# The second FFN with its activations stationary and 512 columns of weights moving

## The chip, the cores and the metric

The kernel runs on one core of one Trainium2 chip. The metric is the device time of one execution in microseconds (us); three runs of the kernel before lie between 2185.66 and 2185.99 us, median 2185.8.

TensorE (PE) multiplies: it loads a stationary block of up to 128x128 and streams the columns of a moving operand past it into PSUM. VectorE (DVE) and ScalarE (ACT) work elementwise on 128 partitions, GpSimd (POOL) hardly computes here, and SyncE (SP) issues transfers.

## The reference

One layer of a decoder for 16 meta tokens and 256 tokens (T = 272, D = 2048) in float32: a half-step FFN, a mixer (sparse attention and a gated convolution), and a second half-step FFN. The output has only the 256 tokens. The change is in the second FFN:

```
def rms_norm(x, g):
    y = x * rsqrt(mean(x * x, axis=-1) + EPS)
    return y * g

def swiglu(x, w_gate, w_up, w_down):           # (2048, 5632), (2048, 5632), (5632, 2048)
    return (silu(x @ w_gate) * (x @ w_up)) @ w_down

u = rms_norm(h, ffn2_norm_g)
h = h + 0.5 * swiglu(u, w_gate, w_up, w_down)
return h[:, N_META:]
```

## The kernel before

All activations lie feature-major: `h` is [128 features, 16 blocks of features, 272 tokens]. Each float32 product is made of three: weights and activations are each split into a rounded high part and the rest (`whi`, `wlo`; hi and lo of `act` or `mid`), and hi x hi, hi x lo and lo x hi are added up in PSUM.

The weights come through one stream (`Stream`, lines 61 to 151). Each transfer on SP's queue brings 128 x 2048 floats (1 MB) into one of three raw buffers. A transfer is split in two *steps* of 1024 columns: ScalarE copies the high part (line 108) and VectorE subtracts (line 109) into one of four buffers. `next()` hands out blocks; when a step's blocks are used up it first runs what is due (`early`), one entry of `steps`, then issues the split three steps ahead, then the work put off with `later(fn, lag)`. So the order on each engine is the order in which this Python code issues it, and the steps are its clock.

In the FFNs (`ffn`, lines 378 to 429) the weights are stationary, 128x128 at a time, and the tokens move. In the second one `paired` (lines 273 to 278) sends `whi` against hi and lo of 256 tokens in one matmul of 512 columns, then `wlo` against hi in one of 256, so the two halves of a PSUM tile have to be added by ScalarE and VectorE (`joined`, `add_to`). The 5632 middle features are done in two halves of 22 blocks: for each block a gate tile `pg` and an up tile `pu` (16 blocks of weights each), then, for each of 16 output blocks, `pd` over 22 blocks. The last `pd` uses three matmuls of 256 columns instead (`fmajor`). The mean of squares is summed by TensorE (`norm`, lines 339 to 366, with lag 2) while the first matmuls run on activations that are not yet normalised; `R` is multiplied in afterwards. Finished blocks of `h` go out on POOL's queue, or on SP's once every load is issued (line 928).

The index projection in the mixer already does it the other way round: `tokens` (lines 483 to 495) holds a tile of 128 tokens stationary and moves 512 columns of weights, so that PSUM gets [tokens, features] (`pi`, `pq`).

Of the kernel before, what the change touches and what calls it, by code (L numbers as in the profile page):

```python
# [9 lines left out]
F32 = mybir.dt.float32  # L10
F32R = mybir.dt.float32r
# [7 lines left out]
FF = 5632  # L19
NF = FF // P  # L20
FHALF = NF // 2
SEQ = 256
META = 16
T = META + SEQ
# [130 lines left out]
def tile_decoder_layer(  # L155
# [36 lines left out]
    def ffn_chunks(wgu, wd, skip=0):  # L192
        for c in range(2):
            chunks(wgu, max(skip, c * 2 * FHALF), (c + 1) * 2 * FHALF)
            chunks(wd, c * FHALF, (c + 1) * FHALF)

    st.add(wgu1[0], RAW // P, P, (4, 8))
    ffn_chunks(wgu1, wd1, 1)
    chunks(wk, 0, G)
    st.add(wkw, KD, NKW)  # L200
    chunks(wv, 0, G)
# [3 lines left out]
    chunks(wgc, 0, KD * 3 // 2)  # L205
    chunks(wga, 0, KD * 3 // 2)
    chunks(wo, 0, KD)
    ffn_chunks(wgu2, wd2)

    const.tile([P, 32], F32, name="lead")  # L210
    h = const.tile([P, KD, T], F32, name="h")
# [38 lines left out]
    def mm_tile(name="mm"):  # L250
        return psum.tile([P, 512], F32, name=name, tag="mm")
# [15 lines left out]
    def fmajor(ps, xhi, xlo, n):  # L267

        for k in range(n):
            whi, wlo = st.next()  # L270
            mac(ps, whi, wlo, xhi(k), xlo(k), k == 0, k == n - 1)

    def paired(ps, x, n):

        for k in range(n):
            whi, wlo = st.next()
            nc.tensor.matmul(ps.rearrange("p (a t) -> p a t", a=2), whi, x(k), start=k == 0, stop=False)  # L277
            nc.tensor.matmul(ps[:, :SEQ], wlo, x(k)[:, 0, :], start=False, stop=k == n - 1)  # L278

    def joined(out, ps):  # L280
# [17 lines left out]
    def parts(at):  # L298

        return (lambda k, c0=0, c1=T: act[:, k, 0, at + c0 : at + c1]), (  # L300
            lambda k, c0=0, c1=T: act[:, k, 1, at + c0 : at + c1]
        )

    def next_act(d, gain, c0, at):

        x = h[:, d, c0:]
        g = gain[:, d : d + 1]
        hi, lo = (f(d, c0) for f in parts(at))
        nc.scalar.activation(hi, x, AF.Copy, scale=g)
        nc.vector.scalar_tensor_tensor(lo, x, g, hi.bitcast(F32), op0=ALU.mult, op1=ALU.subtract)  # L310
# [64 lines left out]
                mac(ps[:, :n], whi, wlo, xhi(k), xlo(k), k == 0, k == KD - 1)  # L375
        return four

    def ffn(c0, at, done, wait, starting):
        n = T - c0
        a_hi, a_lo = parts(at)  # L380
        pitch = PITCH if n > SEQ else SEQ
        with tc.tile_pool(name=f"ffn{c0}", bufs=2, reuse_waits="tile") as fp:
            mid = fp.tile([P, FHALF, 2, pitch], F32R, name="mid", bufs=1)
            i_hi, i_lo = (mid[:, :, i, pitch - n :] for i in range(2))
            xhi, xlo = (lambda k: a_hi(k, c0)), (lambda k: a_lo(k, c0))
            pairs = n == SEQ

            def up(ps):
                if pairs:
                    paired(ps, lambda k: act[:, k, :, at + c0 : at + T], KD)  # L390
                else:
                    fmajor(ps[:, :n], xhi, xlo, KD)

            def down(ps, last):
                if pairs and not last:
                    paired(ps, lambda k: mid[:, k, :, :], FHALF)
                else:
                    fmajor(ps[:, :n], lambda k: i_hi[:, k, :], lambda k: i_lo[:, k, :], FHALF)

            def normed(out, ps):  # L400
                if pairs:
                    joined(out, ps)
                    nc.vector.tensor_mul(out, out, R[:, c0:])
                else:
                    nc.vector.tensor_mul(out, ps[:, :n], R[:, c0:])

            def gate(pg, box):
                box["t"] = fp.tile([P, n], F32, name="t")
                normed(box["t"], pg)

            def silu(box):
                box["s"] = fp.tile([P, n], F32, name="s")
                nc.scalar.activation(box["s"], box["t"], AF.Silu)

            def times(pu, box):
                box["v"] = fp.tile([P, n], F32, name="v")
                normed(box["v"], pu)
                nc.vector.tensor_mul(box["v"], box["v"], box["s"])

            norm(c0, wait, mm_tile("norm"))  # L420
            least = st.at + wait + 1
            for c in range(2):
                for f in range(FHALF):
                    box = {}
                    side = int(starting and c == 0 and f < 2)
                    if side:
                        if f == 0:
                            four = start_tiles(n, xhi, xlo)
                        pg, pu = four[2 * f : 2 * f + 2]
                    else:  # L430
                        pg, pu = mm_tile("pg"), mm_tile("pu")
                        up(pg)
                    st.later(lambda pg=pg, box=box: gate(pg, box), 1, least)
                    st.later(lambda box=box: silu(box), 2, least + 1)
                    if not side:
                        up(pu)
                    st.later(lambda pu=pu, box=box: times(pu, box), 1 + side, least + 1)
                    st.later(lambda f=f, box=box: split_into(i_hi[:, f, :], i_lo[:, f, :], box["v"]), 2 + side, least + 2)
                for d in range(KD):
                    pd = mm_tile("pd")  # L440
                    last = d == KD - 1 and c == 1
                    down(pd, last)
                    st.later(lambda d=d, pd=pd, last=last: add_to(h[:, d, c0:], pd, 0.5, pairs and not last))
                    if c == 1:
                        done(d)
            if not starting:
                st.flush()

# [9 lines left out]
    for d in range(KD):  # L458
        st.later(lambda d=d: square(d, 0), 4 + d * 7 // KD)

    def done1(d):
        st.later(lambda: (next_act(d, gains[1], 0, LATER), square(d, 0)), 2)

    ffn(0, LATER, done1, 10, True)


    with ExitStack() as mix:
# [15 lines left out]
        def tokens(ps_of, tts):  # L483

            k = 0
            while k < KD:
                blocks = [st.next()] + st.rest()
                for j in tts:
                    t0, n = TT[j]
                    for i, (whi, wlo) in enumerate(blocks):  # L490
                        xhi, xlo = a_hi(k + i, t0, t0 + n), a_lo(k + i, t0, t0 + n)
                        nc.tensor.matmul(ps_of[j], xhi, whi, start=k + i == 0, stop=False)
                        nc.tensor.matmul(ps_of[j], xhi, wlo, start=False, stop=False)
                        nc.tensor.matmul(ps_of[j], xlo, whi, start=False, stop=k + i == KD - 1)
                k += len(blocks)

        steps = st.steps

# [113 lines left out]

        for i in range(2):
            pi = {j: mm_tile(f"pi{j}") for j in (1, 2)}
            tokens(pi, (1, 2))
# [198 lines left out]

        for i in range(2):
            pq = {j: mm_tile(f"pq{j}") for j in (1, 2)}
            tokens(pq, (1, 2))
# [106 lines left out]
            st.later(lambda d=d: (next_act(d, gains[2], META, LATER), square(d, META)), 2)  # L924


    def done2(d):
        st.later(lambda: (nc.sync if st.n_loaded == len(st.loads) else nc.gpsimd).dma_start(out[d], h[:, d, META:]))

    ffn(META, LATER, done2, 2, False)  # L930


_INS = [
# [26 lines left out]

def _down(w):
    return _chunks(np.concatenate([_tiles(w[: FF // 2], P), _tiles(w[FF // 2 :], P)]))


def _branch(gate, w):
# [26 lines left out]
def _layout(x, meta_tokens, ffn1_norm_g, ffn1_w_gate, ffn1_w_up, ffn1_w_down, mix_norm_g, w_in, q_norm_g,  # L992
# [31 lines left out]
    a["wgu2"] = _pairs(ffn2_w_gate[0], ffn2_w_up[0])  # L1024
    a["wd2"] = _down(ffn2_w_down[0])
    return a


# [17 lines left out]
```

## Time and profile before

| | us |
|---|---|
| three runs, median | 2185.8 |
| the profiled execution | 2185.66 |
| its span, from the first to the last instruction | 2183.9 |
| second FFN, first to last matmul | 1446.4 to 2180.7 |
| TensorE busy | 2175.9 |
| VectorE busy | 1317.1 |
| ScalarE busy | 1015.4 |

In the profile PE is the matmuls and PEld the loads of stationary blocks, which overlap. A row of a timeline gives the start, the length and the engine, then line, operation, output <- inputs and shape, and in brackets the idle time before it and what ended that. Matmuls are pipelined: each lasts longer than the distance to the next, so distances are read from starts. Rows of groups give count, busy time, mean duration in ns and the idle time before.

### The profile page before, as it was taken

The page shows a single profiled execution, that of the slowest core. Times are in us where ns is not written, and L with a number is a line of the kernel's source. Part 1 is how long each engine was busy: PE and PEld are TensorE (multiplying, and loading weights), DVE is VectorE, ACT ScalarE, POOL GpSimd, SP SyncE. Part 2 cuts the span into 40 slices and gives each one's busy share as a digit, 9 for nine tenths or more (in the row PEclk, how much of TensorE's full clock was granted, in tenths as well). Part 3 has the DMA queues.
Part 4 walks back from the last instruction along what each step waited for, and adds up shares of the span by engine and source line. Part 5 has one row for each costly group of instructions (what it writes and reads, how often), then busy time and mean ns, then how long its engine had stood idle before and what let it go on. Part 6 is the DMA issues. An engine that isn't in the chain of part 4 may idle for free.

```text
span 2183.9 us, 34927 instructions
## 1 busy us (share of the span) xinstructions
PE 2175.9 (100%) x14554; PEld 2002.7 (92%) x14554; DVE 1317.1 (60%) x1848; ACT 1015.4 (46%) x1460; POOL 15.4 (1%) x26
## 2 busy tenths in 40 slices
PE   9999999999999999999999999999999999999999
PEld 9999999999999998898988888888888888888888
DVE  7555544455555555686566677676666556666654
ACT  6444433344444445564444555554444444444443
POOL 0000000000000000000000000000000000000000
PEclk9999999999999999999999999999999999999999
DMA  6555455545555445443455555555555555555553
GB/s 248 195 185 176 174 177 183 181 174 175 179 185 176 174 167 182 163 157 135 174 184 184 189 186 184 193 175 192 193 193 188 183 192 190 193 193 190 187 205 132
DMA packets 56894, 397.89 MB, mean 182 GB/s; under 512 B 6560, under 2 KB 7712, under 8 KB 9248
## 3 DMA queue, kind: packets, MB, share of 16 engines
q1 hardware_dynamic: 55872, 393.95, 51.2%
q8 instruction: 114, 1.87, 0.3%
q0 software_dynamic: 576, 1.57, 0.2%
q14 instruction: 44, 0.36, 0.0%
q10 hardware_dynamic: 288, 0.15, 0.0%
HBM read 393.54 MB, written 2.10 MB: 181 GB/s over the span
## 4 chain that ended last, share of the span: by engine, by line
PE 96%; DVE 2%; ACT 1%; DMA 1%; issue 0%; ACTq 0%; DVEq 0%
PE pu L277 7%; PE pg L277 7%; PE pd L277 7%; PE pgt L277 6%; PE pd L264 4%; PE pd L263 4%; PE pd L265 4%; PE pu L263 4%; PE pu L265 4%; PE pu L264 4%; PE pg L263 4%; PE pg L265 4%; PE pg L264 4%; PE pu L278 4%; PE pg L278 4%; PE pd L278 4%
## 5 line engine op out<-in xcount | busy, mean ns | idle before, releaser
L109 DVE TENSOR_TENSOR wlo<-raw,whi 128x1024 fp32r<-128x1024 f32 (+1 forms) x747 | 912.9, 1222 | 794.2 <-ACT whi L108 793.4
L108 ACT ACTIVATE whi<-raw 128x1024 fp32r<-128x1024 f32 (+1 forms) x747 | 788.5, 1056 | 985.8 <-issue 159.9
L277 PE MATMUL pg<-act,whi 128*128 128x512 f32 x704 | 246.3, 394 | 0.4 <-DVE act L310 0.4
L277 PE MATMUL pu<-act,whi 128*128 128x512 f32 x704 | 246.2, 394 | 0.0
L277 PE MATMUL pd<-mid,whi 128*128 128x512 f32 x682 | 236.5, 394 | 0.0
L263 PE MATMUL pd<-mid,whi 128*128 128x272 f32 (+1 forms) x726 | 207.9, 286 | 0.0
L265 PE MATMUL pd<-mid,wlo 128*128 128x272 f32 (+1 forms) x726 | 207.9, 286 | 0.0
L264 PE MATMUL pd<-mid,whi 128*128 128x272 f32 (+1 forms) x726 | 207.9, 286 | 0.0
L278 PE MATMUL pg<-act,wlo 128*128 128x256 f32 x704 | 195.1, 277 | 0.0
L278 PE MATMUL pu<-act,wlo 128*128 128x256 f32 x704 | 195.0, 277 | 0.0
L263 PE MATMUL pg<-act,whi 128*128 128x272 f32 x672 | 192.7, 287 | 0.0
L264 PE MATMUL pg<-act,whi 128*128 128x272 f32 x672 | 192.5, 287 | 0.0
L265 PE MATMUL pu<-act,wlo 128*128 128x272 f32 x672 | 192.5, 287 | 0.0
L264 PE MATMUL pu<-act,whi 128*128 128x272 f32 x672 | 192.5, 287 | 0.0
L265 PE MATMUL pg<-act,wlo 128*128 128x272 f32 x672 | 192.5, 287 | 0.0
L263 PE MATMUL pu<-act,whi 128*128 128x272 f32 x672 | 192.5, 287 | 0.0
L278 PE MATMUL pd<-mid,wlo 128*128 128x256 f32 x682 | 188.9, 277 | 0.0
L277 PE MATMUL pgt<-act,whi 128*128 128x512 f32 x512 | 182.2, 398 | 0.0
L277 PEld LDWEIGHTS pg<-act,whi 128*128 128x128 f32 x704 | 132.0, 188 | 31.4 <-DVE act L310 0.7
L277 PEld LDWEIGHTS pu<-act,whi 128*128 128x128 f32 x704 | 132.0, 188 | 30.6
L277 PEld LDWEIGHTS pd<-mid,whi 128*128 128x128 f32 x682 | 127.9, 188 | 29.7
L278 PE MATMUL pgt<-act,wlo 128*128 128x256 f32 x512 | 143.8, 281 | 0.0
(214 smaller groups left out, 4040.2 us busy)
## 6 DMA issues: line engine op xcount, KB each, us to landing
raw<-in_wgu_dram SPq DMA_DIRECT2D x175, 1024.0 KB, 4.8
raw<-in_wd_dram SPq DMA_DIRECT2D x88, 1024.0 KB, 4.9
raw<-in_wcv_dram SPq DMA_DIRECT2D x24, 1024.0 KB, 4.8
raw<-in_wgc_dram SPq DMA_DIRECT2D x24, 1024.0 KB, 4.7
raw<-in_wga_dram SPq DMA_DIRECT2D x24, 1024.0 KB, 4.7
raw<-in_wo_dram SPq DMA_DIRECT2D x16, 1024.0 KB, 4.8
raw<-in_wqi_dram SPq DMA_DIRECT2D x8, 1024.0 KB, 4.8
raw<-in_wq_dram SPq DMA_DIRECT2D x8, 1024.0 KB, 4.7
```

What stands on the lines that cost most here:

```text
L108: nc.scalar.activation(hi[:, :n], raw, AF.Copy)
L109: nc.vector.tensor_sub(lo[:, :n], raw, hi[:, :n].bitcast(F32))
L263: nc.tensor.matmul(ps, whi, xhi, start=first, stop=False)
L264: nc.tensor.matmul(ps, whi, xlo, start=False, stop=False)
L265: nc.tensor.matmul(ps, wlo, xhi, start=False, stop=last)
L277: nc.tensor.matmul(ps.rearrange("p (a t) -> p a t", a=2), whi, x(k), start=k == 0, stop=False)
L278: nc.tensor.matmul(ps[:, :SEQ], wlo, x(k)[:, 0, :], start=False, stop=k == n - 1)
```

## The change

In the second FFN the activations become stationary and the weights move. `tokens` is lifted out of the mixer and takes any operand: for each step of two 128x512 weight blocks and each of two tiles of 128 tokens, three matmuls of 512 columns per block. Gate, up and down results are now [tokens, features]. So:

- the weights are laid out on the host in tiles of 512 columns; the middle features are done in groups of 6 and then 5 times 512, each group with its own down projection;
- the norm's factor belongs to a partition (`rcol`): ScalarE applies it with Silu straight from PSUM, VectorE in one product with the gate;
- the product `s` [tokens, 512 features] must become [features, tokens] to be stationary for the down projection: VectorE turns squares of 32x32 (`STREAM_TRANSPOSE`), 16 instructions of 32 partitions x 256 for each 512 features, over four steps; then `mid` is split as before;
- the residual `h` is turned the same way into `ht` [tokens, 2048] by 32 instructions of 32 partitions x 512, one at each of 32 steps from the fifth on;
- the output leaves as [tokens, features] in eight transfers of 256 KB, the last ones on SP's and ScalarE's queues.

```diff
+GROUPS = 6, 5
...
+    def tokens(ps_of, x, n):
+        k = 0
+        while k < n:
+            blocks = [st.next()] + st.rest()
+            for j, ps in ps_of.items():
+                for i, (whi, wlo) in enumerate(blocks):
+                    xhi, xlo = x(k + i, j, 0), x(k + i, j, 1)
+                    nc.tensor.matmul(ps, xhi, whi, start=k + i == 0, stop=False)
+                    nc.tensor.matmul(ps, xhi, wlo, start=False, stop=False)
+                    nc.tensor.matmul(ps, xlo, whi, start=False, stop=k + i == n - 1)
+            k += len(blocks)
...
+    def turned(dst, src, rows, cols):
+        nc.vector.transpose(dst[rows * 32 : rows * 32 + 32], src[cols * 32 : cols * 32 + 32])
+
+    def ffn_tokens():
...
+            st.steps.extend([lambda: None] * 4)
+            st.steps.extend(lambda j=j, q=q, r=r: turn_h(j, q, r) for j in range(2) for q in range(4) for r in range(4))
...
+            st.later(lambda: nc.vector.tensor_add(ssq[0][:, META:], ssq[0][:, META:], ssq[1][:, META:]), 2)
+            st.early(across, 3)
+            st.later(root, 3)
+            st.later(inverse, 4)
...
+            def gate(pg, s):
+                for j in (1, 2):
+                    nc.scalar.activation(s[:, j - 1], pg[j], AF.Silu, scale=rcol[:, 2 * j : 2 * j + 1])
+
+            def times(pu, s):
+                for j in (1, 2):
+                    nc.vector.scalar_tensor_tensor(
+                        s[:, j - 1], pu[j], rcol[:, 2 * j : 2 * j + 1], s[:, j - 1], op0=ALU.mult, op1=ALU.mult
+                    )
+
+            def turn_s(mt, s, r):
+                for q in range(4):
+                    turned(
+                        mt.rearrange("p f (j r b) -> p r j f b", j=2, r=4)[:, r],
+                        s.rearrange("p j (f q b) -> p q j f b", f=4, q=4)[:, q],
+                        q, r,
+                    )
+
+            def add(d, j, pd, last):
+                to = ht[:, j - 1, d * 512 : (d + 1) * 512]
+                nc.vector.scalar_tensor_tensor(to, pd, 0.5, to, op0=ALU.mult, op1=ALU.add)
+                if last:
+                    queue = nc.gpsimd if st.n_loaded < len(st.loads) else (nc.sync, nc.scalar)[j - 1]
+                    queue.dma_start(out[j - 1, :, d * 512 : (d + 1) * 512], to)
+
+            for c, n in enumerate(GROUPS):
+                for f in range(n):
...
+                    tokens(pg, act_tokens, KD)
+                    st.later(lambda pg=pg, s=s: gate(pg, s))
+                    pu = {j: mm_tile(f"pu{j}") for j in (1, 2)}
+                    tokens(pu, act_tokens, KD)
+                    st.later(lambda pu=pu, s=s: times(pu, s))
+                    for r in range(4):
+                        st.later(lambda mt=mt, s=s, r=r: turn_s(mt, s, r), 2 + r)
+                    to = mid[:, 4 * f : 4 * f + 4]
+                    st.later(lambda to=to, mt=mt: split_into(to[:, :, 0], to[:, :, 1], mt), 6)
+                for d in range(D // 512):
+                    pd = {j: mm_tile(f"pd{j}") for j in (1, 2)}
+                    tokens(pd, lambda k, j, part: mid[:, k, part, (j - 1) * P : j * P], 4 * n)
+                    for j in (1, 2):
+                        st.later(lambda d=d, j=j, ps=pd[j], c=c: add(d, j, ps, c == 1))
```

On TensorE, at the start of the second FFN, the order before (`po` is the end of the output projection):

```order
L277 MATMUL po<-ms_13662,whi 128x512
L278 MATMUL po<-ms_13662,wlo 128x256
L277 MATMUL pg<-act,whi 128x512
L278 MATMUL pg<-act,wlo 128x256
L277 MATMUL pg<-act,whi 128x512
L278 MATMUL pg<-act,wlo 128x256
```

And now, at the same place (two `pg` tiles, one for each 128 tokens):

```order
L290 MATMUL pg_14727<-whi,act 128x512
L291 MATMUL pg_14727<-wlo,act 128x512
L292 MATMUL pg_14727<-whi,act 128x512
L290 MATMUL pg_14727<-whi,act 128x512
L291 MATMUL pg_14727<-wlo,act 128x512
L292 MATMUL pg_14727<-whi,act 128x512
L290 MATMUL pg_14728<-whi,act 128x512
L291 MATMUL pg_14728<-wlo,act 128x512
L292 MATMUL pg_14728<-whi,act 128x512
```

Pairs of 512 and 256 columns give way to matmuls of 512 columns alone, six in a row for each token tile. On VectorE, the order before for one block of 128 middle features:

```order
L283 TENSOR_TENSOR t<-pg,u 128x256
L403 TENSOR_TENSOR t<-t,R 128x256
L109 TENSOR_TENSOR wlo<-raw,whi 128x1024 x2
L283 TENSOR_TENSOR v<-pu,u 128x256
L403 TENSOR_TENSOR v<-v,R 128x256
L418 TENSOR_TENSOR v<-v,s 128x256
L109 TENSOR_TENSOR wlo<-raw,whi 128x1024
L296 TENSOR_TENSOR mid<-v,mid 128x256
```

And now, after the second 512 middle features, where the last turns of the residual (`ht`) still lie between:

```order
L483 SCALAR_TENSOR_TENSOR s<-pu_15204,rcol,s 128x512
L483 SCALAR_TENSOR_TENSOR s<-pu_15205,rcol,s 128x512
L446 STREAM_TRANSPOSE ht<-h 32x16x32
L110 TENSOR_TENSOR wlo<-raw,whi 128x1024
L446 STREAM_TRANSPOSE mt<-s 32x2x4x32 x4
L446 STREAM_TRANSPOSE ht<-h 32x16x32
L110 TENSOR_TENSOR wlo<-raw,whi 128x1024
L446 STREAM_TRANSPOSE mt<-s 32x2x4x32 x4
L446 STREAM_TRANSPOSE ht<-h 32x16x32
L110 TENSOR_TENSOR wlo<-raw,whi 128x1024
L446 STREAM_TRANSPOSE mt<-s 32x2x4x32 x4
```

The work on the middle features has moved from every block of 128 to a burst after each 512, and between two weight splits stand five turns now.

## Rows read from the trace of the kernel before

**Rows 1.** The page: TensorE's busy time, and the clock row of 40 slices.
```profile
PE 2175.9 (100%) x14554; PEld 2002.7 (92%) x14554; DVE 1317.1 (60%) x1848; ACT 1015.4 (46%) x1460; POOL 15.4 (1%) x26
...
PEclk9999999999999999999999999999999999999999
```

**Rows 2.** Second FFN: length, busy us (count) of PE, PEld, DVE, ACT, POOL; clock, DMA.
```profile
1446.39:2180.71 734.32, 733.64 (x4250) 641.91 (x4248) 449.43 (x600) 340.03 (x474) 6.65 (x12) 1.00 0.53 187
```

**Rows 3.** Timeline, TensorE (start us, us): end of output projection, second FFN.
```profile
1440.03 0.40 PE L277 MATMUL po<-ms,whi 128*128 128x512 f32 x1
...
1446.39 0.40 PE L277 MATMUL pg<-act,whi 128*128 128x512 f32 x1
...
1599.95 0.39 PE L277 MATMUL pu<-act,whi 128*128 128x512 f32 x1
...
1603.42 0.39 PE L277 MATMUL pg<-act,whi 128*128 128x512 f32 x1
...
2180.07 0.28 PE L265 MATMUL pd<-mid,wlo 128*128 128x256 f32 x1
```

**Rows 4.** Timeline, TensorE, index projection: two starts 75 matmuls apart.
```profile
833.10 0.39 PE L492 MATMUL pi<-whi,act 128*128 128x512 f32 x1
...
850.10 0.39 PE L492 MATMUL pi<-whi,act 128*128 128x512 f32 x1
```

**Rows 5.** Groups by shape, TensorE (count, busy us, mean ns, idle before).
```profile
L277 PE MATMUL pg<-act,whi 128*128 128x512 f32 x704 | 246.3, 394 | 0.4 <-DVE act L310 0.4
...
L277 PE MATMUL pu<-act,whi 128*128 128x512 f32 x704 | 246.2, 394 | 0.0
...
L277 PE MATMUL pd<-mid,whi 128*128 128x512 f32 x682 | 236.5, 394 | 0.0
...
L263 PE MATMUL pd<-mid,whi 128*128 128x256 f32 x22 | 6.2, 283 | 0.0
```

**Rows 6.** Groups by shape, VectorE.
```profile
L109 DVE TENSOR_TENSOR wlo<-raw,whi 128x1024 fp32r<-128x1024 f32 x743 | 909.8, 1225 | 792.2 <-ACT whi L108 791.5
...
L292 DVE TENSOR_TENSOR h<-h,u 128x256 f32<-128x256 f32 x47 | 20.0, 425 | 22.4 <-ACT u L291 22.4
...
L770 DVE COPY pTm<-ppt 16x256 f32<-16x256 f32 x8 | 3.3, 410 | 1.2 <-ACT pTx L769 0.9
...
L296 DVE TENSOR_TENSOR ys<-ppv,ys 128x512 fp32r<-128x512 f32 x4 | 2.8, 691 | 2.9 <-ACT ys L295 2.9
...
L331 DVE RECIPROCAL rs_y<-rs_z 128x256 f32<-128x256 f32 x1 | 1.7, 1744 | 0.0
```

**Rows 7.** Groups by shape, ScalarE.
```profile
L108 ACT ACTIVATE whi<-raw 128x1024 fp32r<-128x1024 f32 x743 | 785.8, 1059 | 982.4 <-issue 159.9 <-PE pd L264 144.4 <-PE pg L264 141.9
...
L413 ACT ACTIVATE s<-t 128x256 f32<-128x256 f32 x44 | 17.7, 403 | 1.6 <-DVE t L403 1.6
...
L530 ACT ACTIVATE zz<-pi,rcol 128x512 f32<-128x512 f32 x4 | 2.5, 674 | 0.0
```

**Rows 8.** Timeline, all engines, around the sum of squares.
```profile
1452.26 0.50 PE L277 MATMUL pg<-act,whi 128*128 128x512 f32 x1 [0.41 <-DVE act L310]
...
1452.57 0.43 DVE L344 TENSOR_TENSOR ssq<-ssq,ssq 128x256 f32<-128x256 f32 x1
...
1453.15 0.67 PE L348 MATMUL norm<-ssq,ones 128*128 128x256 f32 x2 [0.27 <-DVE ssq L344]
```

**Rows 9.** Timeline, all engines, the end.
```profile
2180.43 0.28 PE L265 MATMUL pd<-mid,wlo 128*128 128x256 f32 x1
...
2180.74 0.42 DVE L288 SCALAR_TENSOR_TENSOR h<-pd,h 128x256 f32<-128x256 f32 x1 [6.54 <-PE pd L265]
...
2181.20 0.33 SPq L928 DMA_DIRECT2D out_dram<-h  x1
```

**Rows 10.** DMA issues (KB each, median us to landing).
```profile
raw<-in_wgu_dram SPq DMA_DIRECT2D x175, 1024.0 KB, 4.8
...
out_dram<-h SPq DMA_DIRECT2D x4, 128.0 KB, 1.7
```

More of the change, by code (lines that the diff above doesn't have):

```diff
@@ L190, in chunks @@
             st.add(src[i], RAW // width, width)
[L192 to L195, printed above, removed]
     st.add(wgu1[0], RAW // P, P, (4, 8))
-    ffn_chunks(wgu1, wd1, 1)
+    for c in range(2):
+        chunks(wgu1, max(1, c * 2 * FHALF), (c + 1) * 2 * FHALF)
+        chunks(wd1, c * FHALF, (c + 1) * FHALF)
     chunks(wk, 0, G)
@@ L207, in tile_decoder_layer @@
     chunks(wo, 0, KD)
-    ffn_chunks(wgu2, wd2)
+    gu = down = 0
+    for n in GROUPS:
+        chunks(wgu2, gu, gu + 8 * n, 512)
+        chunks(wd2, down, down + 4 * n, 512)
+        gu, down = gu + 8 * n, down + 4 * n
     const.tile([P, 32], F32, name="lead")
@@ L278, in paired, with act_tokens @@
             nc.tensor.matmul(ps[:, :SEQ], wlo, x(k)[:, 0, :], start=False, stop=k == n - 1)
+    def tokens(ps_of, x, n):
[9 more added lines that the diff above has]
+            k += len(blocks)
+    def act_tokens(k, j, part):
+        t0, n = TT[j]
+        return act[:, k, part, LATER + t0 : LATER + t0 + n]
     def joined(out, ps):
@@ L376, in start_tiles, with ffn_features @@
         return four
[L378 to L405, printed above, removed]
+    def ffn_features():
+        n = T
+        xhi, xlo = parts(LATER)
+        with tc.tile_pool(name="ffn1", bufs=2, reuse_waits="tile") as fp:
+            mid = fp.tile([P, FHALF, 2, PITCH], F32R, name="mid", bufs=1)
+            i_hi, i_lo = (mid[:, :, i, PITCH - n :] for i in range(2))
             def gate(pg, box):
                 box["t"] = fp.tile([P, n], F32, name="t")
-                normed(box["t"], pg)
+                nc.vector.tensor_mul(box["t"], pg[:, :n], R)
             def silu(box):
@@ L424, in ffn @@
                     box = {}
-                    side = int(starting and c == 0 and f < 2)
+                    side = int(c == 0 and f < 2)
                     if side:
@@ L440, in ffn @@
                     pd = mm_tile("pd")
-                    last = d == KD - 1 and c == 1
-                    down(pd, last)
-                    st.later(lambda d=d, pd=pd, last=last: add_to(h[:, d, c0:], pd, 0.5, pairs and not last))
+                    fmajor(pd[:, :n], lambda k: i_hi[:, k, :], lambda k: i_lo[:, k, :], FHALF)
+                    st.later(lambda d=d, pd=pd: add_to(h[:, d], pd, 0.5, False))
                     if c == 1:
-                        done(d)
-            if not starting:
-                st.flush()
+                        st.later(lambda d=d: (next_act(d, gains[1], 0, LATER), square(d, 0)), 2)
@@ new lines, in turned, with turn_h, across @@
+    def turned(dst, src, rows, cols):
+        nc.vector.transpose(dst[rows * 32 : rows * 32 + 32], src[cols * 32 : cols * 32 + 32])
+    def ffn_tokens():
+        with tc.tile_pool(name="ffn2", bufs=1, reuse_waits="tile") as fp:
+            ht = fp.tile([P, 2, D], F32, name="ht")
+            mid = fp.tile([P, 4 * GROUPS[0], 2, SEQ], F32R, name="mid")
+            def turn_h(j, q, r):
+                to = ht[:, j].rearrange("p (f b) -> p f b", b=P)
+                at = META + j * P + q * 32
+                turned(to[:, :, r * 32 : r * 32 + 32], h[:, :, at : at + 32], q, r)
+            st.steps.extend([lambda: None] * 4)
+            st.steps.extend(lambda j=j, q=q, r=r: turn_h(j, q, r) for j in range(2) for q in range(4) for r in range(4))
+            ps = aux_tile("norm")
+            def across():
+                for j in (1, 2):
+                    t0 = TT[j][0]
+                    nc.tensor.matmul(
+                        ps[:, 0, 2 * j : 2 * j + 2], ssq[0][:, t0 : t0 + P], ones[:, :2], start=True, stop=True
+                    )
+            root, inverse = rsqrt(rcol[:, 2:6], ps[:, 0, 2:6], (P, 4), 1.0 / D)
+            st.later(lambda: nc.vector.tensor_add(ssq[0][:, META:], ssq[0][:, META:], ssq[1][:, META:]), 2)
[16 more added lines that the diff above has]
+                        q, r,
+                    )
+            def add(d, j, pd, last):
[6 more added lines that the diff above has]
+                for f in range(n):
+                    s = fp.tile([P, 2, 512], F32, name="s", bufs=2)
+                    mt = fp.tile([P, 4, SEQ], F32, name="mt", bufs=2)
+                    pg = {j: mm_tile(f"pg{j}") for j in (1, 2)}
+                    tokens(pg, act_tokens, KD)
[10 more added lines that the diff above has]
+                    tokens(pd, lambda k, j, part: mid[:, k, part, (j - 1) * P : j * P], 4 * n)
+                    for j in (1, 2):
+                        st.later(lambda d=d, j=j, ps=pd[j], c=c: add(d, j, ps, c == 1))
+            st.flush()
@@ L481, in tile_decoder_layer @@
         zk = [mp.tile([P, G * HD + NKW], F32, name=f"zk{j}") for j in range(3)]
[L483 to L495, printed above, removed]
         steps = st.steps
@@ L924, in tile_decoder_layer @@
             st.later(lambda d=d: (next_act(d, gains[2], META, LATER), square(d, META)), 2)
[L927 to L930 removed]
+    ffn_tokens()
 _INS = [
@@ L1023, in _layout @@
     a["wo"] = _tiles(w_out[0], P)
-    a["wgu2"] = _pairs(ffn2_w_gate[0], ffn2_w_up[0])
-    a["wd2"] = _down(ffn2_w_down[0])
+    gu = np.stack([_tiles(ffn2_w_gate[0], 512), _tiles(ffn2_w_up[0], 512)], 1)
+    a["wgu2"] = _chunks(gu.reshape(-1, P, KD * 512))
+    a["wd2"] = _down_columns(ffn2_w_down[0])
     return a
@@ L1044 @@
     got = np.asarray(r.results[0]["out_0_dram"])
-    return np.ascontiguousarray(got.reshape(D, SEQ).T).reshape(1, SEQ, D)
+    return got.reshape(1, SEQ, D)
```

23 lines of the change are left out of this document (12 added, 11 removed).

## The prediction

> **What bounds the kernel now.** I read the busy shares first, then the clock row, then the second FFN by itself. TensorE (PE) is busy for 2175.9 of 2183.9 us and the granted clock is full in every slice, which is the 2.4 GHz level [rows 1]. So the kernel takes as long as its matmuls follow one another, and any other engine counts only where TensorE comes to wait for it. In the second FFN, 734.3 us long, TensorE stands idle for 0.7 us, while VectorE (DVE) is busy for 449 us and ScalarE (ACT) for 340 [rows 2]. The durations in the groups (394 ns for 512 columns) overlap and must not be added; what counts is the distance from one start to the next, so I read starts in the timeline. Ten pairs (one matmul of 512 columns, one of 256) go from 1599.95 to 1603.42: 347 ns for a pair [rows 3]. At 2.4 GHz, 768 columns are 320 ns, so each matmul costs some 13.4 ns beside its columns. The counts are 704, 704 and 682 pairs, and 22 times three matmuls of 256 columns for the last tile [rows 5]; a matmul of 256 columns stands 0.12 us from the next (three from 2180.07 to 2180.43 [rows 3, 9]), 13.3 over its columns too. 2090 x 0.347 + 66 x 0.12 = 733 us, which is the stage.
>
> **The matmuls.** The new loop sends, for each 128x512 block of weights, three matmuls of 512 columns for each of two token tiles. 2112 blocks of 128x128 are 528 such blocks, so 3168 matmuls with 1,622,016 columns. The old form has 2112 x 768 = 1,622,016 columns: exactly as many. Nothing is saved on columns; what goes is 4246 - 3168 = 1078 matmuls. What a matmul of the new form takes stands in the trace, since the index projection (pi) uses the same loop, the same weight buffers and the same stationary activations: 75 starts in 17.00 us, 226.7 ns each, 13.3 over the 213.3 of its columns [rows 4]. That stretch had VectorE at work too, and the distance was the same throughout. 3168 x 0.2267 = 718.1 us. Against 733.1 this is 15.0 us less.
>
> The Trainium skill ("TensorE: Matmul & The Clock Gate", "Wait — 56ns, not 53.3ns?") gives a fixed cost of about 2.5 ns per warm matmul in place of the 13.4. By it the 1078 matmuls would be worth 2.7 us. The trace disagrees in both forms, and the sum goes by the trace.
>
> **The start of the stage.** TensorE sums the squares across partitions ahead of the third step of 1024 weight columns (a step is 12 matmuls, 2.72 us). The sum waits for VectorE's last adds, which ended at 1453.0 and let TensorE start at 1453.15 [rows 8]; nothing in the chain before it is changed. Two steps end at 1446.39 + 5.44 = 1451.83, so TensorE stands for 1.3 us, and the two tiny matmuls take about 0.35. Before, the waits and the sum in this place came to about 1 us, so the first block falls back by some 0.6 us. The wait for the last activation (it held the sixteenth block) goes: the new loop comes to it 19 us after the start. The stage's last matmul then starts at 1446.39 + 718.1 - 0.2 + 1.65 = 2165.9, where it was 2180.43: 14.5 us earlier.
>
> **The end.** The last matmul is 0.11 us longer (0.39, not 0.28), the last add has 512 columns and not 256 (0.69 for 0.42 [rows 6, 9]), and two transfers of 256 KB go out on two queues where one of 128 KB did. From 128 KB in 1.7 us and 1024 KB in 4.8 [rows 10], 128 KB more are 0.44 us; the other half, 1.4 us ahead, may cost as much again, I take 0.4. The tail grows by 1.2 us. An output transfer now stands on ScalarE's queue with six weight copies behind it; it waits for an add about 1 us, and there are three steps of cover. The POOL queue issues 4 transfers in place of 12, long before the end.
>
> **What VectorE and ScalarE are asked.** For 512 middle features VectorE did 4 x 2.54 = 10.1 us (six operations of about 0.42 [rows 6]) beside the weight splits. It now does two products of 0.69 [rows 6], sixteen turns and one split of 1.23, so the total depends on the turn, an operation that the trace does not show. Bounds: columns alone, as the copy of 16 partitions x 256 (0.41) and an addition in SBUF (0.425); from above, the slowest operation of 256 columns, the reciprocal, 1.74 [rows 6]. I take 0.43 for 256 columns and 0.69 for the 512 of the residual, since three kinds of operation and two partition counts lie there and only the reciprocal, an iterated one, lies far away.
>
> The Trainium skill ("Vector Engine (DVE) Microarchitecture Reference", 3.8 "The reshape front-end and per-opcode configuration") says that the turning array sustains one element per cycle per lane. By it my estimate for the turn stays near the addition's time; no row here shows it.
>
> Does TensorE then wait? ScalarE and VectorE need 1.06 + 1.23 = 2.3 us for a step's weights [rows 6, 7], there are four buffers, and a buffer is free again three steps (8.16 us) before it is needed: a cushion of 5.9 us. For each 512 features there is a burst of six steps: the products, four steps with four turns t, the split. It overdraws 6 x 1.225 + 1.38 + 1.23 + 16t - 16.32 = 16t - 6.36: 0.5 us at t = 0.43. In the first burst a residual turn T lies in each of the six steps too: 0.5 + 6 x 0.69 = 4.7 us, still inside the cushion, by 1.2 us. In the second three such turns are left; the other nine have none. ScalarE's share (two Silu of about 0.7 from PSUM [rows 7]) fits beside one weight copy in a step of 2.72. The products wait for TensorE's last up matmul, with turns and weight splits behind them; that delay is in the burst. The last middle tile is ready two to four steps before the down projection comes to it. So I cost all this at nothing; if the cover is gone, see the first rival.
>
> **Sum.** -14.5 + 1.2 = -13.3 us on a profiled execution of 2185.66 us (span 2183.9); that lies 0.1 us under the median of the runs, so 2172.4 us against 2185.8.
>
> **Rivals.**
> *A turn takes longer than its columns.* For it: no row shows one, squares are filled before they can be emptied, and each starts in other partitions than the one before. Against: every plain operation of this width lies at 0.41 to 0.43. The first burst loses 16t - 6.36 + 6T - 5.9, the second the same with 3T, the other nine 16t - 12.3 where that is positive. At two cycles a column (t = 0.69, T = 1.22): 6.1 + 2.4 + 0 = 8.5 us, 2181.
> *On the other side: the turns bound the up projection.* With t = 0.78, T = 1.4 the loss is 8.6 + 4.4 + 2 = 15 us and the gain is gone; from there each 0.1 us costs about 20. At three cycles a column (0.96, 1.76) it is 14 + 8 + 28 = 50 us, 2222; at the reciprocal's 1.74 over 200 us, near 2375. TensorE would stand before matmuls on wlo from the second group of 512 features on.
> *The distance of matmuls is not a constant.* The same pair took 353 ns up to 1446.39 (18 from 1440.03) and 347 after [rows 3], so something in the stage's rhythm is worth 3.3 ns a matmul. In the worse state the new loop would take 10.5 us more: 2183, no change that can be told. In a state better by as much: 2162. Against both: the index projection stood at 226.7 while the pairs around it were in the worse state.
> *The excess goes with the columns, not with the matmul.* Then the same columns take the same 733 us, and the tail and the start make the kernel 1.8 us slower: 2187.5, still no change that can be told. Against: 256 and 512 columns carry the same 13.3 ns [rows 3, 4].
>
> By the 2.5 ns of the Trainium skill's page on TensorE, named above, that rival would come out at 2184.8.
>
> **Chances.** Forecast (2170 to 2176) 0.68; turns partly uncovered (2176 to 2184) 0.10; turns as the bound 0.08; worse distance 0.07; better distance 0.05; excess with the columns 0.02. The range 2167 to 2184 leaves out the bound by turns and the better distance, and a little besides. A difference under 0.2% (4.4 us, about what a measurement of this kernel can tell from no change) is "same": the worse distance, the excess with the columns and a part of the uncovered turns. Faster 0.82, same 0.09, slower 0.09.
>
> **What would show it.** In the profile of the changed kernel the starts of matmuls in the second FFN should lie 226.7 ns apart, in up and down alike, some 1078 matmuls fewer, and the stage should last about 720 us. The 176 turns of the middle should take 0.41 to 0.45 us and the 32 of the residual about 0.7. TensorE's only wait should be the 1.3 us at the sum of squares, with none on wlo between 45 and 70 us into the stage, where the first burst lies. The tail from the last matmul's start to the end should grow from 3.4 to about 4.6 us. I am wrong if TensorE waits for VectorE, or if the distance is not 226.7.

## The result and the profile after

The changed kernel takes 2172.07 us (median of four runs, 2172.04 to 2172.45), the kernel before 2185.86 in the runs beside it: a ratio of 0.9937, with a 95% interval of 0.992 to 0.9955, so it is faster by some 0.6%. 2172.4 us was forecast. The span of the profiled execution is 2170.7 us, where it was 2183.9. Ratios leave out two executions that lie far off: one of the kernel before at 2866.3 us (granted clock 0.697) and one of the run with both edits at 5214.77 us (full clock).

The page and the second FFN after, answering to [rows 1, 2] (length, then busy us and count of PE, PEld, DVE, ACT, POOL, clock, DMA):

```profile
PE 2160.4 (100%) x13478; PEld 1955.1 (90%) x13478; DVE 1324.3 (61%) x1778; ACT 979.4 (45%) x1286; POOL 11.1 (1%) x18
...
PEclk9999999999999999999999999999999999999999
```

```profile
1446.84:2166.88 720.04, 719.04 (x3174) 594.98 (x3172) 456.18 (x530) 303.63 (x300) 2.33 (x4) 1.00 0.56 190
```

TensorE has as little idle time as before, at full clock; it has 1076 matmul records fewer (1078 fewer in the products, two more in the sum of squares), and the stage lasts 720.0 us in place of 734.3. VectorE is as busy as it was, 456 us against 449. The starts, answering to [rows 3, 4]: the first and the last of the stage, and two pairs of starts that lie 75 matmuls apart, one from a gate tile to an up tile and one in the down projection.

```profile
1446.84 0.40 PE L290 MATMUL pg<-whi,act 128*128 128x512 f32 x1
...
1600.28 0.39 PE L290 MATMUL pg<-whi,act 128*128 128x512 f32 x1
...
1617.28 0.39 PE L290 MATMUL pu<-whi,act 128*128 128x512 f32 x1
...
1800.20 0.39 PE L290 MATMUL pd<-whi,mid 128*128 128x512 f32 x1
...
1817.20 0.39 PE L290 MATMUL pd<-whi,mid 128*128 128x512 f32 x1
...
2166.49 0.39 PE L292 MATMUL pd<-whi,mid 128*128 128x512 f32 x1
```

17.00 us for 75 matmuls is 226.7 ns each, as in the index projection, and the down projection has the same distance. The new operations of VectorE in the groups by shape (count, busy us, mean ns, idle before):

```profile
L446 DVE STREAM_TRANSPOSE mt<-s 32x256 f32<-32x256 f32 x176 | 76.7, 436 | 2.8
...
L446 DVE STREAM_TRANSPOSE ht<-h 32x512 f32<-32x512 f32 x32 | 22.5, 703 | 0.9
...
L483 DVE SCALAR_TENSOR_TENSOR s<-pu,rcol,s 128x512 f32<-128x512 f32 x22 | 15.4, 742 | 0.0
```

A turn of 256 columns takes 0.436 us and one of 512 takes 0.703, about as long as an addition of as many columns (0.425 and 0.691 in [rows 6]). The sum of squares and the end, answering to [rows 8, 9]:

```profile
1452.12 0.39 PE L292 MATMUL pg<-whi,act 128*128 128x512 f32 x1
...
1453.50 0.61 PE L467 MATMUL norm<-ones,ssq 128*128 128x2 f32 x4 [0.99 <-DVE ssq L472]
```

```profile
2166.91 0.69 DVE L497 SCALAR_TENSOR_TENSOR ht<-pd,ht 128x512 f32<-128x512 f32 x1 [0.67 <-PE pd L292]
...
2167.64 0.35 ACTq L500 DMA_DIRECT2D out_dram<-ht  x1
```

The 0.99 us before `norm` is the only wait of TensorE in the stage. At the end, 0.69 us of the last addition and 3.0 us from the issue on ScalarE's queue to the end of the span stand where 0.42 and 2.7 stood.

Between the two profiles, the first matmul of the stage starts 0.45 us later (1446.84 for 1446.39, ahead of all that was changed), the stage from its first to its last matmul's start is 14.39 us shorter (719.65 for 734.04), and the tail from there is 0.7 us longer (4.2 for 3.5). Together that is the 13.2 us by which the spans differ. Where the 0.45 us come from was not looked into.

### The profile page after: what moved, and what is told of

Same layout as the page of the kernel before. It is cut to its first block, busy times and chain, and to the rows that moved or that the text cites. A ratio compares the mean times of both kernels' runs of the same rounds, so it can differ in the third digit from the quotient of the medians.

```text
span 2170.7 us, 32296 instructions
## 1 busy us (share of the span) xinstructions
PE 2160.4 (100%) x13478; PEld 1955.1 (90%) x13478; DVE 1324.3 (61%) x1778; ACT 979.4 (45%) x1286; POOL 11.1 (1%) x18
## 4 chain that ended last, share of the span: by engine, by line
PE 96%; DVE 2%; ACT 1%; DMA 1%; issue 0%; ACTq 0%; DVEq 0%
PE pgt L279 6%; PE pd L265 4%; PE pd L267 4%; PE pd L266 4%; PE pu L267 4%; PE pu L266 4%; PE pu L265 4%; PE pg L267 4%; PE pg L266 4%; PE pg L265 4%; PE pu L292 4%; PE pd L290 4%; PE pd L291 4%; PE pu L291 4%; PE pu L290 4%; PE pd L292 4%
## 5 line engine op out<-in xcount | busy, mean ns | idle before, releaser
L265 PE MATMUL pd<-mid,whi 128*128 128x272 f32 x704 | 201.7, 287 | 0.0
L266 PE MATMUL pd<-mid,whi 128*128 128x272 f32 x704 | 201.7, 287 | 0.0
L267 PE MATMUL pd<-mid,wlo 128*128 128x272 f32 x704 | 201.7, 287 | 0.0
L290 PE MATMUL pg<-whi,act 128*128 128x512 f32 x352 | 137.1, 389 | 0.0
L291 PE MATMUL pg<-wlo,act 128*128 128x512 f32 x352 | 136.9, 389 | 0.0
L292 PE MATMUL pg<-whi,act 128*128 128x512 f32 x352 | 136.9, 389 | 0.0
L290 PE MATMUL pu<-whi,act 128*128 128x512 f32 x352 | 136.9, 389 | 0.0
L290 PE MATMUL pd<-whi,mid 128*128 128x512 f32 x352 | 136.9, 389 | 0.0
L292 PE MATMUL pd<-whi,mid 128*128 128x512 f32 x352 | 136.9, 389 | 0.0
L292 PE MATMUL pu<-whi,act 128*128 128x512 f32 x352 | 136.9, 389 | 0.0
L291 PE MATMUL pu<-wlo,act 128*128 128x512 f32 x352 | 136.9, 389 | 0.0
L291 PE MATMUL pd<-wlo,mid 128*128 128x512 f32 x352 | 136.9, 389 | 0.0
```

The source lines that it names most:

```text
L265: nc.tensor.matmul(ps, whi, xhi, start=first, stop=False)
L266: nc.tensor.matmul(ps, whi, xlo, start=False, stop=False)
L267: nc.tensor.matmul(ps, wlo, xhi, start=False, stop=last)
L290: nc.tensor.matmul(ps, xhi, whi, start=k + i == 0, stop=False)
L291: nc.tensor.matmul(ps, xhi, wlo, start=False, stop=False)
L292: nc.tensor.matmul(ps, xlo, whi, start=False, stop=k + i == n - 1)
```

## The experiments

The theory was: the second FFN is a row of matmuls that never waits, each costs 13.3 ns beside its columns, and VectorE's new work is hidden because its bursts fit into the cushion of weights that are split ahead. The rivals were that the excess goes with the columns, that VectorE's new work costs or gains time somewhere, and that the distance of matmuls hangs on something else. The ratios below are to the kernel before, in the runs beside each. Some of these executions of the kernel before take 2199.5 to 2200.3 us and not 2186 (see the phase of the pairs); ratios with such runs among them lie up to 0.3% lower than the medians make them, so between experiments I compare the medians.

**Matmuls cut in half.** The changed kernel:

```diff
-nc.tensor.matmul(ps, xhi, whi, ...)          # and xhi, wlo and xlo, whi
+for c in (0, 256):                           # but for the first of each PSUM tile
+    nc.tensor.matmul(ps[:, c : c + 256], xhi, whi[:, c : c + 256], ...)
```

> The changed kernel with each matmul of the second FFN cut in two of 256 columns, but for the first of each of the 60 PSUM tiles: 3108 matmuls more, the same columns, the same operands. Theory (each matmul costs 13.3 ns beside its columns): 3108 x 13.3 ns = 41 us more than the changed kernel, about 2213 us, starts 120 ns apart. Rival (the excess goes with the columns, and the gain came from something else, such as the adding up of halves that went): no change from the changed kernel, 2172. By the 2.5 ns per matmul of the Trainium skill ('TensorE: Matmul & The Clock Gate', 'Wait — 56ns, not 53.3ns?') it would be 8 us more, 2180.

Measured: 2213.89 us, ratio 1.0122 (1.0099 to 1.0145). The page:

```profile
PE 2202.0 (100%) x16586; PEld 2117.5 (96%) x16586; DVE 1324.8 (60%) x1778; ACT 979.4 (44%) x1286; POOL 11.1 (1%) x18
```

These are 3108 matmuls more than the 13478 above, and 41.8 us more than the changed kernel: 13.5 ns for each. The rival that the excess goes with the columns is out, and the 2.5 ns that the Trainium skill ("TensorE: Matmul & The Clock Gate", "Wait — 56ns, not 53.3ns?") gives do not hold for these matmuls. Each of them has a load of its own stationary block, here as before (PEld has the same count as PE, x16586), so whether the 13.5 ns belong to the matmul or to its load was not told apart.

**The kernel before in matmuls of 256 columns.**

```diff
-            pairs = n == SEQ
+            pairs = False
```

> The kernel before with the second FFN in three matmuls of 256 columns per block instead of 512 and 256; the adding up of two halves by ScalarE and VectorE goes with it. Columns are the same, 2090 matmuls more. Theory: 2090 x 13.3 ns = 28 us slower than before, about 2213 us. Rival (the excess goes with the columns, or adding up the halves cost time): no change from before or a little faster, 2186 or less.

Measured: 2214.06 us, ratio 1.0122 (1.0096 to 1.0149). Two starts in its timeline, 34 blocks (102 matmuls) apart:

```profile
1599.72 0.28 PE L263 MATMUL pg<-act,whi 128*128 128x256 f32 x1
...
1611.96 0.28 PE L263 MATMUL pg<-act,whi 128*128 128x256 f32 x1
```

12.24 us for 102 matmuls is 120 ns, 13.3 over the 106.7 of 256 columns. 28.2 us for 2090 matmuls more is 13.5 ns each, in the old roles of weights and activations too; that here the adding up of two halves was gone gave nothing back. So it is the number of matmuls (each with its load) that counts, and not which operand stands still.

**No turns of the middle.** The split reads the product as it lies, so the down projection multiplies unturned data:

```diff
-for r in range(4):
-    st.later(lambda mt=mt, s=s, r=r: turn_s(mt, s, r), 2 + r)
+mt = s.rearrange("p j (a b) -> p (j a) b", b=SEQ)
```

> The changed kernel without the turns of the middle: the split reads the product as it lies, so the down projection multiplies unturned data. The residual is still turned. Theory (all turns are hidden behind matmuls): no change, 2172 within 0.5 us. Rival (they slow the matmuls, through the memory they share or by late weight splits): several us faster, up to the 77 us that they are busy.

Measured: 2172.15 us, 0.1 from the changed kernel. VectorE's busy time fell by 74 us (1250.0 for 1324.3) and nothing came of it: the turns of the middle are hidden.

**Turns of the middle twice, turns of the residual twice.** Two runs, in each of which the same instruction is issued a second time:

```diff
-for q in range(4):                  # in turn_s
+for q in (0, 0, 1, 1, 2, 2, 3, 3):
```

> The changed kernel with each of the 176 turns of the middle done twice (the second writes the same values). With the 0.436 us that the profile of the changed kernel shows for one, a burst of six steps now overdraws VectorE by 7.6 us against a cushion of 5.9. Theory (what counts is the burst against the cushion): 6 us lost in the first, 4 in the second, 1.8 in each of nine others, 26 us; up to 40 if ScalarE's copies, which wait behind the split of the middle, are held up as well: 2198 to 2212. Rival (VectorE's mean load counts; 456 + 77 us busy of 719): no change, 2172.

```diff
-turned(to[...], h[...], q, r)       # in turn_h
+for _ in range(2):
+    turned(to[...], h[...], q, r)
```

> The changed kernel with each of the 32 turns of the residual done twice. They lie in the first two bursts alone. With 0.703 us for one, the first burst overdraws VectorE by 0.7 + 8.4 = 9.1 us against the cushion of 5.9. Theory (the cushion was nearly used up): 3 us lost, up to 9 if ScalarE's copies are held up as well: 2175 to 2181, with TensorE waiting on wlo near 1500 us. Rival (there is far more cover than that): no change, 2172.

Measured: 2226.15 us and 2182.18 us, 54.1 and 10.1 more than the changed kernel, where 26 to 40 and 3 to 9 were expected. The mean load of VectorE is out as what counts; the bursts are right in kind, and my price for overrunning the cushion was too small. Who waited for whom in the first of the two (total us, times, longest):

```profile
PE pu L291 <- DVE wlo L110: 18.2, 9, 2.7
...
PE pg L291 <- DVE wlo L110: 9.3, 11, 2.5
...
ACT mid L314 <- DVE mt L446: 102.1, 11, 11.5
```

TensorE's waits in the stage come to 33 us, nearly all of them for `wlo`. The last row looks like a cause, since the split of the middle on ScalarE waits for the turns with the next weight copies behind it (in the changed kernel itself that wait is 3.9 us at most). But it held up nothing that these waits were for. VectorE, ScalarE and TensorE in one of the later bursts:

```profile
1607.27 1.23 DVE L110 TENSOR_TENSOR wlo<-raw,whi 128x1024 fp32r<-128x1024 f32 x1
1608.53 3.67 DVE L446 STREAM_TRANSPOSE mt<-s 32x256 f32<-32x256 f32 x8
1612.23 1.23 DVE L110 TENSOR_TENSOR wlo<-raw,whi 128x1024 fp32r<-128x1024 f32 x1
1613.48 3.69 DVE L446 STREAM_TRANSPOSE mt<-s 32x256 f32<-32x256 f32 x8
1617.20 1.23 DVE L110 TENSOR_TENSOR wlo<-raw,whi 128x1024 fp32r<-128x1024 f32 x1
...
1607.28 1.06 ACT L109 ACTIVATE whi<-raw 128x1024 fp32r<-128x1024 f32 x1 [1.66 <-DVE mt L446]
1617.21 1.06 ACT L314 ACTIVATE mid<-mt 128x1024 fp32r<-128x1024 f32 x1 [8.87 <-DVE mt L446]
...
1613.51 0.50 PE L291 MATMUL pg<-wlo,act 128*128 128x512 f32 x1 [0.60 <-DVE wlo L110]
...
1618.48 0.50 PE L291 MATMUL pu<-wlo,act 128*128 128x512 f32 x1 [1.94 <-DVE wlo L110]
```

VectorE works without a gap, and the copy for the split at 1617.20 is the one of 1607.28, done 8.9 us earlier. So it is in all 23 waits for `wlo` in this run: the copy was done 6.4 to 12.2 us before VectorE came to the split. Only at the end of the last group does TensorE wait for the split of the middle itself (2.0 and 0.6 us). What my price had too small is VectorE's own work. From one split to the next, with eight turns between, it needs 4.96 us, where the durations add up to 1.23 + 8 x 0.436 = 4.72; over the four such steps of a burst that is 1.0 us, and a later burst costs TensorE 2.9 us from start to start, not 1.8.

The rest is the clock and slow starts. The first line is the whole run; of the other two, one is a stretch in which TensorE was busy for 2.31 of 5.00 us, and one the stretch behind it (columns as in [rows 2]; the clock stands behind the five engines):

```profile
core 0: 2223.7 us, clock 0.994
```

```profile
1515.00:1520.00 5.00, 2.31 (x11) 1.60 (x10) 4.80 (x10) 2.12 (x3) 0.00 (x0) 1.00 0.60 210
...
1520.00:1523.00 3.00, 3.00 (x8) 2.36 (x9) 2.92 (x4) 2.92 (x4) 0.00 (x0) 0.53 0.01 3
```

At 0.53 the second stretch is almost wholly at the 1.2 GHz level. The starts of the timeline give the whole sum. In the profiled execution the stage lasts 773.3 us from its first start to its last, 53.6 more than in the changed kernel. The 25 stops, counted from start to start, are 37.3 us of it. 59 distances of about 427 ns in place of 226.7, at the lower clock, are 11.7. The first distances behind a stop (335 to 343 ns at full clock) and the slightly longer ones after them are the remaining 4.6.

In the second run the waits on wlo were 7.5 us, in two groups of 512 features where the residual's turns lie:

```profile
PE pg L291 <- DVE wlo L110: 5.1, 4, 1.5
...
PE pu L291 <- DVE wlo L110: 2.4, 2, 1.5
```

Here too the copies were done long before (3.3 to 10.4 us). Half of the waits lie in the second group, where I had expected none, because between the two bursts the cushion does not come back. With two turns of the residual a step keeps VectorE busy for 2.73 us, as long as TensorE takes for a step (2.72):

```profile
1522.37 1.23 DVE L110 TENSOR_TENSOR wlo<-raw,whi 128x1024 fp32r<-128x1024 f32 x1
1523.63 1.44 DVE L446 STREAM_TRANSPOSE ht<-h 32x512 f32<-32x512 f32 x2
1525.10 1.22 DVE L110 TENSOR_TENSOR wlo<-raw,whi 128x1024 fp32r<-128x1024 f32 x1
```

**The sum of squares two steps later.**

```diff
-st.early(across, 3); st.later(root, 3); st.later(inverse, 4)
+st.early(across, 5); st.later(root, 5); st.later(inverse, 6)
```

> The changed kernel with the sum of squares across partitions two steps later on TensorE (ahead of the fifth step, not the third). Theory (TensorE's only wait in the stage, 0.99 us, is for the last adds of squares; the factor itself is needed only after eight steps): 1.0 us faster than the changed kernel, 2171.0. Rival (what follows the sum is then late and gives it back): no change.

Measured: 2170.82 us (2170.44 to 2171.08), 1.25 less than the changed kernel. The wait is gone from TensorE's timeline:

```profile
1457.46 0.50 PE L467 MATMUL norm<-ones,ssq 128*128 128x2 f32 x4
```

**The phase of the pairs.** In the merge and the output projection of both kernels pairs of 512 and 256 columns follow each other at 353.3 ns; in the second FFN of the kernel before the same pairs took 346.7. First came one tiny matmul ahead of the merge, with nothing to wait for:

```diff
+px = aux_tile("px")
+nc.tensor.matmul(px[:, 0, :2], ones, ones[:, :2], start=True, stop=True)
 for branch, merge in ((conv_out, conv_merge), (attn_out, attn_merge)):
```

> The changed kernel with one tiny matmul (2 columns) between the convolution and the gates of the merge, 365 us ahead of the second FFN. Pairs of 512 and 256 columns follow each other there at 353.3 ns, in a pattern of three (349, 350, 361), and in the second FFN of the kernel before at 346.6, in a pattern of two (343, 350), with the same operands. Theory (the distance hangs on the phase in which the stream of matmuls was last started): the pairs fall into the better pattern, 1024 x 6.6 ns = 6.8 us faster, 2165.4; or a restart without a pause keeps the old one, 2172.2. Rival (the distance belongs to the stage, by its operands or by what the other engines do): no change.

Measured: 2172.18 us; the distances stayed at 353.3. It decided nothing, since a restart that lands in the same pattern is what either theory allows. Then with a wait:

```diff
+def pause():
+    nc.scalar.activation(w2, ones[:, :2], AF.Copy)
+    nc.tensor.matmul(px[:, 0, :2], ones, w2, start=True, stop=True)
+st.later(pause)
```

> As the run with a tiny matmul, but the matmul waits for a value that ScalarE writes behind the next weight copy, so that TensorE stands for some 1.3 us before it starts again, as it did at the start of the second FFN of the kernel before. Theory of the phase: 6.8 - 1.3 = 5.5 us faster, 2166.6, if the better pattern is hit; 1.3 slower if not. Rival (the distance belongs to the stage): 1.3 us slower, 2173.4.

Measured: 2171.59 us median, but from 2171.14 to 2178.11, two executions of six near 2178 and four from 2171.14 to 2171.99. The profile is of one of the two. TensorE stood for 3.75 us, not 1.3, and then ran at 1.2 GHz, from about 1089.4 to 1092.5 (start us, us; then windows as above):

```profile
1088.34 0.27 PE L972 MATMUL px<-w,ones 128*128 128x2 f32 x1 [3.75 <-ACT w L971]
```

```profile
1089.00:1090.00 1.00, 1.00 (x6) 0.80 (x5) 0.00 (x0) 0.00 (x0) 0.00 (x0) 0.57 0.98 410
...
1090.00:1091.00 1.00, 1.00 (x5) 0.90 (x4) 0.00 (x0) 0.00 (x0) 0.00 (x0) 0.50 0.99 418
...
1093.00:1094.00 1.00, 1.00 (x8) 0.86 (x7) 0.00 (x0) 0.86 (x1) 0.00 (x0) 1.00 0.00 0
```

Its pairs were at 353.3 again. The four others were not profiled. They took some 6.7 us less, at the same granted clock on record (0.998 to 0.999, as in the two), and the better pattern would be worth 6.8; so one program seems to have run in either pattern, which is argued and not shown. So the pause was made short and of two lengths, by sending a value from TensorE to ScalarE and back, once and twice:

```diff
+def trips():
+    nc.tensor.matmul(px[:, 0, :2], ones, ones[:, :2], start=True, stop=True)
+    for i in range(n):                                    # n = 1 and n = 2
+        nc.scalar.activation(w2[:, i], px[:, i % 2, :2], AF.Copy)
+        nc.tensor.matmul(px[:, (i + 1) % 2, :2], ones, w2[:, i], start=True, stop=True)
+st.early(trips)
```

> The changed kernel with a short pause of TensorE ahead of the gates of the merge: a tiny matmul, a copy of its result by ScalarE, a tiny matmul on that copy; about 0.8 us without matmuls of the merge, short enough to keep the granted clock. (The run with a longer pause stood for 3.75 us and fell to half the clock for 3.4 us in its profile, 2177.7; four of its six executions took 2171.2, though.) Theory of the phase: the pairs of the merge and of the output projection fall into the pattern of two (346.6 ns) and the run takes 2172.1 + 0.8 - 6.8 = 2166; or, where the new phase is again the bad one, 2172.9. Rival (the distance belongs to the stage): 2172.9.

> As the run with one round trip, with two of them, a pause of about 1.5 us: another phase. Theory of the phase: 2172.1 + 1.5 - 6.8 = 2166.8 if this one is hit, 2173.6 if not. Rival (the distance belongs to the stage): 2173.6, and the runs with one and with two trips differ by 0.7 us alone.

Measured: 2172.99 us (2172.82 to 2173.2) with one trip and 2166.69 us (2166.56 to 2166.88) with two; the ratios are 0.9913 and 0.9884 (0.9852 to 0.9916). The gates of the merge began 0.65 us later with two trips than with one (the tiny matmuls that end the trips, first the one, then the second):

```profile
1085.32 0.38 PE L974 MATMUL px<-w,ones 128*128 128x2 f32 x2 [0.26 <-ACT w L973]
1085.97 0.38 PE L974 MATMUL px<-w,ones 128*128 128x2 f32 x2 [0.26 <-ACT w L973]
```

Two starts 30 pairs apart in the merge, first of the changed kernel, then with two trips:

```profile
1200.22 0.40 PE L279 MATMUL pgt<-act,whi 128*128 128x512 f32 x1
...
1210.82 0.40 PE L279 MATMUL pbr<-cs,whi 128*128 128x512 f32 x1
```

```profile
1200.01 0.39 PE L279 MATMUL pbr<-cs,whi 128*128 128x512 f32 x1
...
1210.41 0.39 PE L279 MATMUL pbr<-cs,whi 128*128 128x512 f32 x1
```

10.60 us against 10.40: 353.3 ns a pair against 346.7, with the same operands and, but for one tiny copy, the same work on the other engines. A pause 0.65 us longer made the program 6.3 us faster, and the distance stayed so to the end of the output projection. So it does not belong to the stage; it hangs on how the row of matmuls was last started, which I call its phase. What the phase consists of is not shown. Nor is it one of two states alone: the single distances are 346, 347 and 347 ns here, where those of the kernel before are 350 and 343 in turn, with the same mean.

The kernel before shows the same in its own profile. Its 14 pairs from 1446.39 on, already in the second FFN, still take 353.6 ns each, and 346.7 comes only behind the two short waits of [rows 8]:

```profile
1451.34 0.40 PE L277 MATMUL pg<-act,whi 128*128 128x512 f32 x1
```

This also gives a reading of its times: of its 48 runs beside these experiments 13 stand at 2199.5 to 2200.3 us, at the same granted clock (0.999 to 1.0), and all others but one from 2185.6 to 2186.5. Between the two lie some 13.8 us, and 2090 pairs at 6.6 ns more (353.3 for 346.7) are 13.8 us. None of the 13 was profiled, so that is argued and not shown. By it the changed kernel, whose four runs agree within 0.4 us, gains twice as much against those executions.

**Both edits that helped.** The later sum of squares and two round trips.

> The changed kernel with both edits that helped: two round trips ahead of the merge's gates, and the sum of squares two steps later. Theory: the two gains lie in different places and add: 2166.7 - 1.2 = 2165.5. Rival (the later sum takes away a restart on which the second FFN's rhythm hangs, or moves another phase): the gain of one of them is lost, 2166.7 or more.

Measured: 2165.67 us (four of five executions from 2165.38 to 2165.7), ratio to the kernel before 0.9906 (0.9891 to 0.9921): the two gains add, and this is faster than both kernels.

## Why the prediction was right

*What bounds the kernel* and *the matmuls* were right, the second to its number: 226.7 ns were taken from the index projection and 226.7 were found, in all three products. That the 13.4 ns go with the number of matmuls, each with its load, was shown by cutting them, in both forms; it was the term on which the whole gain rested.

*The start* was right: the one wait is there, and moving the sum gave 1.25 us back. The profile's 0.99 us count from the end of a matmul; counted as the forecast counts, from where the next start would have come, the wait is 1.15 us for the 1.3 forecast. The sum itself is four tiny matmuls and not two, 0.47 us for 0.35, so that 1.62 stand against 1.65. The stage from first to last start was forecast at 719.5 us and took 719.65.

*The end* was taken too dear: 1.2 us forecast, 0.7 measured. From the issue to the end of the span it is 0.3 us more than before, so the 0.4 us that I had put down for a disturbance of the two transfers did not come.

That the spans differ by 13.2 us for the forecast 13.3 is partly luck: the first start fell 0.45 us later, which nothing in the forecast had, and the end came 0.5 us cheaper.

*What VectorE is asked* was right at the value taken (0.43 and 0.69 forecast, 0.436 and 0.703 measured; 0.69 and 0.742 for the products). That it costs nothing was shown by leaving out the turns of the middle, and by the profile, where TensorE waits for nothing but the sum of squares. The estimate by the Trainium skill ("Vector Engine (DVE) Microarchitecture Reference", 3.8 "The reshape front-end and per-opcode configuration") agrees with the 0.436. The cover is there, though thinner than forecast. The tightest split of the stage, in the first burst:

```profile
1514.77 1.23 DVE L110 TENSOR_TENSOR wlo<-raw,whi 128x1024 fp32r<-128x1024 f32 x1
...
1516.86 0.39 PE L291 MATMUL pu<-wlo,act 128*128 128x512 f32 x1
```

It ends 0.9 us before TensorE's matmul on it starts, where 1.2 were forecast. The nine later bursts leave 4.6 us where 5.4 were forecast; without the turns of the middle most steps have 5.9, which is the forecast cushion. So the working of the first rival was too kind: it added up durations, where VectorE's instructions start somewhat further apart, let the cushion come back in full from one burst to the next, and left out that waits of TensorE cost clock and slow starts. Doubling the turns cost 54 us where that working gave 26, and doubling the residual's cost 10 where it gave 3. The point from which the turns would have eaten the gain lies lower than the 0.78 us that I gave; how much lower was not measured.

*The rival on the distance of matmuls* did not come about here, but what it rested on is real: it was worth 6.3 us in the changed kernel, at another place. Its reading of the rows, 353 ns up to 1446.39 and 347 after, put the change at the start of the stage; it lies 5 us later, behind the waits. That the new loop stood at 226.7 ns at every place looked at, behind either pattern, is seen, not explained.

## What to carry to other kernels

Where TensorE never waits, count matmuls as well as columns: here the same columns in fewer, wider matmuls gained 13.3 ns for each that went (with its load), and a stretch of the same kernel that already has the new form gives the price. Work that is hidden by a buffer ahead has to be judged in its densest steps and not by its share of the stage: by the distances from start to start rather than by durations, and with a look at whether the steps between two bursts let the buffer fill again.

## What the runs showed of the hardware

- The same row of matmuls can run at two distances: pairs of 512 and 256 columns at 353.3 ns (349, 350, 361 in turn) or at 346.7 (350 and 343, or 346, 347, 347). From the merge on it changes in these profiles, if at all, only behind a stop of TensorE; a stop of one length left it where it was, one 0.65 us longer moved it.
- Behind a stop of TensorE of 3.75 us the matmuls ran at 1.2 GHz, and so they did behind a stretch in which it was busy for 2.31 of 5.00 us. Behind the 0.99 us stop at the sum of squares the clock stayed full.
- A turn of 32 partitions costs VectorE about the same as a plain operation of 128 partitions with as many columns (0.436 us against 0.425 for 256, 0.703 against 0.691 for 512).
- In a row of such turns the starts lie some 0.46 us apart (eight turns last 3.67 us), not 0.436.
